# Attention scores kept negated, masked in PSUM by a product, and exponentiated from there

## The chip, the cores and the metric

The kernel runs on one core of one Trainium2 chip. The metric is the device time of one execution in microseconds. The engines are TensorE (PE in the rows, its weight loads PEld), VectorE (DVE), ScalarE (ACT), GpSimd (POOL) and SyncE (SP, which issues the DMAs). Each takes its own instructions in a fixed order; semaphores tie the engines together.

## The reference

One decoder layer on 512 tokens of width 1024, in float32. After a norm and an input projection, two groups of heads run side by side: an RWKV-7 group (8 heads, a recurrence over the tokens, done in chunks of 64) and a sparse-attention group. Their outputs go through an output projection with a residual, then a SwiGLU feed-forward layer and a final norm. The change is in the sparse-attention group, which has 8 query heads of 64 in two groups of 4, each group with its own keys and values, and three branches per head:

- compressed: 31 window tokens made by a small MLP; token t sees a window if the window ends by t; masked softmax, and zero where no window is valid;
- selected: with 8 blocks of 64 tokens and up to 16 chosen, every block is chosen, so this is plain causal attention;
- window: the last 512 tokens, with 512 tokens in all causal attention too, with other keys and values.

```
s = where(valid, q k^T / 8, -1e30);  p = softmax(s);  o = gate_cmp*o_cmp + gate_sel*o_sel + gate_win*o_win
```

## The kernel before

Tokens are tiled by 128 (t = 0..3). The order of the code is: loads, norm and transposition, sixteen projection jobs with their weights split into a high and a low part, RWKV by token tiles (`stage_a`, `stage_b`, `stage_c`), attention by token tiles, output projection, feed-forward, final norm. The code only lists the work; a planner simulates it while the program is built and gives every engine a fixed order by priority and readiness. So attention is woven together with the RWKV tiles that stand ahead of it in the code, and the first part of the output projection with the last attention tile.

PSUM has eight banks, shared by tags: two "s" (scores, some transposes), two "pj" (transposed probabilities, projections), two "ra" and one "rb" (RWKV, projections), one "o" (attention's outputs). In SBUF the probabilities of four heads lie in one tile `prr`, which every pass over four heads reuses.

For a token tile t with n = 128 (t + 1) keys, attention does this:

- Compressed branch (L947 to L969). Per head one product (L949) with the keys' high and low parts side by side, 64 columns. VectorE adds the mask `cneg` to the one half (L953) and the other half to that (L954), takes the maximum over 32 windows (L955), subtracts it (L956); ACT takes the exponential (L957); VectorE sums, inverts and applies the gate (L958 to L960); POOL multiplies by the validity `cvalid` (L961); VectorE normalizes (L962); TensorE transposes (L965), ACT evacuates (L967), TensorE multiplies by the values (L969).
- Selected and window branches (L971 to L1001), in passes over four heads (x = 0..3). For t = 0 and 1 a pass holds both branches (nb = 2), for t = 2 and 3 one. So there are 2 + 2 + 4 + 4 passes and 48 score banks. Per head: two products into an "s" bank (L980 with the keys' high part, L981 with the low part); per branch VectorE computes -(scores + mask) from PSUM into `prr` and its minimum in one instruction (L986, followed by a read of its accumulator), and ACT takes the exponential in place with that minimum as bias and adds up the row (L987); VectorE inverts the sum (L988); POOL scales by the inverse and the gate (L990); TensorE transposes the blocks into a "pj" bank (L993); ACT evacuates (L997), for x = 3 VectorE (L995).
- When a pass is through, the value products add up in "o" (L1001). The pass's transposed probabilities lie in one of two buffers `ptr`. ACT evacuates "o" (L1002).

The causal mask is `negb`, 512 columns of bf16 made at the start by POOL. An f32 product of two f32 operands runs as two instructions; the operands typed as rounded f32 (the scores' ones) take one; a transpose is one. Every product loads its stationary operand anew.

`q` is scaled by 0.125 as it is rotated (`job_qs`), then split and transposed to `qT` (L921 to L934). The helper lines that recur in the rows: L144 and L146 split weights or activations into parts, L163 to L165 are the three products of a projection.

Of the kernel before, what the change touches and what calls it, by code (L numbers as in the profile page):

```python
# [32 lines left out]
def turn_parts(n, bits=12):  # L33
    """1/(2 pi) as n float32 parts of `bits` bits each."""
    from fractions import Fraction
    pi = Fraction(314159265358979323846264338327950288419716939937510582097494459, 10 ** 62)
    rest, parts, unit = 1 / (2 * pi), [], Fraction(1, 2 ** 14)
    for _ in range(n):
        q = int(rest / unit)
        parts.append(float(q * unit))  # L40
        rest -= q * unit
        unit /= 2 ** bits
    return parts
# [3 lines left out]
def hybrid_layer(ctx: ExitStack, tc: tile.TileContext, x, positions, norm_mix, w_in, mu_shift, w0, w2, a0, a2,  # L47
# [26 lines left out]
    def load(src, n):  # L74
        """src: [(128*blocks), n] rows as [128, blocks, n]."""
# [31 lines left out]
    at = 0  # L107
# [40 lines left out]
    def parts(raw, tags=("whi", "wlo"), pool=False, lo_pool=False):  # L148
        """raw [128, blocks, n] -> hi, lo."""
# [17 lines left out]
    def rstd_of(src, cut=()):  # L167
        """1/sqrt(mean(src^2) + eps) over the free axis of [128, D]."""
# [12 lines left out]
    def norm_transposed(src, gain, hT, lT, halves=False):  # L181
        """src(t): [128, D] of token tile t -> hi, lo [128, KB, S] of the normed transpose; by tiles."""
# [24 lines left out]
    def proj_tile(w, c0, m=128):  # L207
        """channels on partitions: m columns of w from c0 -> PSUM [m, S]."""
# [5 lines left out]
    def proj_tok(w, t, m=1):  # L214
        """tokens on partitions: token tiles from t on, the columns of w -> PSUM [128, m * n]."""
# [8 lines left out]
    def mix(p, j, o, m=128):  # L224
        """token shift: p * (1 - mu) + shift(p) * mu."""
# [5 lines left out]
    def rotate(o, src, tab, scale=1.0):  # L231
        """Rotary on the first 16 of each 64 of src [P, t, n, 64] (PSUM) by tab [P, t, 16] -> o; the rest is copied."""
# [14 lines left out]
    # keeps the tensor engine's clock up while the first loads are on their way  # L247
# [9 lines left out]
    # causal mask: the columns from S - 128 - t are those of the token tile t  # L257
    negb = st([128, S], "negb", dtype=BF16)
    POOL.memset(negb, 0.0)
    POOL.affine_select(negb, negb, pattern=[[-1, S]], compare_op=OP.is_ge, fill=MASK, base=S - 128, channel_multiplier=1)  # L260
# [6 lines left out]
    # A_ab: the rows of a chunk's second half have their columns from its middle on, so that the diagonal blocks come first  # L267
# [15 lines left out]
    DVE.tensor_scalar(cneg, cvalid, -MASK, MASK, op0=OP.mult, op1=OP.add)  # L283
# [83 lines left out]
    # pairs of tokens on the contraction: xk[(q d), a, g, m] = token 2m + q  # L367
# [10 lines left out]
    def job_lat(w):  # L378
        # lora: hi and lo of the weights stacked on the contraction, hi in the half q
# [48 lines left out]
    def gate():  # L428
        """sigmoid(g_lat) @ g2, channels on partitions; the last 32 rows: hi, lo, hi by hi, hi, lo on one contraction."""
# [19 lines left out]
    def rsqrt(o, x):  # L449
        """o = 1/sqrt(x), by Newton's steps from a guess that halves the exponent; x [128, n] is positive."""  # L450
# [60 lines left out]
    def inner(a):  # L511
        """A_ab (a = 0) or A_rb (a = 1), transposed, by chunks, masked."""
# [20 lines left out]
    def solve():  # L533
        """A_ab, and a copy whose 32-blocks are on the partitions."""
# [6 lines left out]
    def solve2():  # L541
        """The inverses of the 32-blocks of I - A_ab."""
# [5 lines left out]
        # the rows are independent of each other: the first ones on one engine, the rest on another  # L548
# [11 lines left out]
    def solve4():  # L560
        """(I - A_ab)^-1, transposed, in the place of A_ab: the diagonal blocks, and their product around the block between."""
# [33 lines left out]
    def tok_pair(w, t):  # L595
        """256 columns of w, token tiles t and t + 1 -> [128 tok, 2, 4, 64] in PSUM."""
# [5 lines left out]
    def job_vt(w):  # L602
        """values of the selected and the window branch, tokens on partitions."""
# [6 lines left out]
    def job_ks(w):  # L610
        """keys of the selected (0) and window (1) branch: kA = hi twice, kB = lo twice, channels on partitions."""
# [30 lines left out]
    def job_qs(half):  # L642
        def f(w):
            if half == 0:
                T["qtok"] = st([128, NT, 8, 64], "b8")
            for t in (0, 2):
                rotate(T["qtok"][:, t:t + 2, 4 * half:4 * half + 4], tok_pair(w, t), tab_pair(t), 0.125)
        return f

    def job_cmp1(a, half):  # L650
        """compression of k (a = 0) or v (a = 1): windows -> hidden, half of the contraction."""
        def f(w):
# [10 lines left out]
            # rows: hi, lo of the windows  # L663
# [8 lines left out]
    def hidden(a, b1):  # L672
        """sum of the two rows, transposed; bias, SiLU."""
# [9 lines left out]
    def compressed():  # L683
        """hidden -> one token per window: keys as hi/lo for the scores, values by heads."""
# [69 lines left out]
    rar, abc, rb, rk_, rv, dend, gate_ = (T[n] for n in ("rar", "abc", "rb", "rk", "rv", "dend", "gate"))  # L754
    # the halves of the partitions hold the chunks; "o" operands hold chunk c in the other half, to share a contraction
# [16 lines left out]
    def stage_a(t):  # L772
# [16 lines left out]
        # token layouts; v is centred over each head, which centres y  # L789
# [96 lines left out]
    def stage_c(t):  # L886
        """group norm (y is centred), bonus, gate."""
# [4 lines left out]
        # the sums of the heads of pair i on the partitions from 32i, 16 times each  # L892
# [47 lines left out]
    for t in range(NT):  # L940
# [3 lines left out]
        # the branches' outputs, gated, add up in one bank: [(parity, d), pair of heads, token]  # L944
        po = ps("o", (128, 4, 128))
        # compressed branch
# [191 lines left out]
```

## Time and profile before

| | us |
|---|---|
| device time, three runs | 787.08, 789.80, 790.96; median 789.8 |
| profiled execution: span from first to last instruction | 780.8 |
| profiled execution: its own total | not recorded; the median lies 9.0 above the span |
| TensorE busy, weight loads | 753.5 (96%), 624.1 (80%) |
| VectorE, ACT, POOL busy | 423.9 (54%), 330.3 (42%), 144.4 (18%) |
| mean granted TensorE clock | 0.986 |
| first compressed score product | starts at 230.3 |
| last value product of attention | starts at 372.3 |

Busy time is the union of an engine's instructions; those of TensorE are pipelined and their ends are modelled, so the starts are read beside it. Positions in time are microseconds from the first instruction.

### The profile page before, as it was taken

What the parts mean: (1) busy time and instruction counts of PE and PEld (TensorE: products, weight loads), DVE (VectorE), ACT (ScalarE), POOL (GpSimd) and SP (SyncE); (2) the same over time, 40 slices, a digit from 0 to 9 for tenths busy, and PEclk for the clock granted to TensorE, in tenths of its full rate; (3) what the DMA queues carried; (4) which work ended last, traced back from release to release, by engine and by line L of the source; (5) the groups of instructions that cost most, each with busy time, mean ns of one, the idle gap of its engine ahead of it and who ended that gap; (6) DMA issues with size and microseconds to landing.
All of it is one profiled execution on the core that took longest, in us unless ns stands there. A gap on an engine that the chain in (4) does not pass through costs nothing.

```text
span 780.8 us, 13178 instructions
## 1 busy us (share of the span) xinstructions
PE 753.5 (96%) x5397; PEld 624.1 (80%) x5397; DVE 423.9 (54%) x902; ACT 330.3 (42%) x592; POOL 144.4 (18%) x244
## 2 busy tenths in 40 slices
PE   7999999998989999989999999999999999999996
PEld 6867788988977878756879888888888888888885
DVE  5486689799678878793474133322222323332235
ACT  6399554234277776475343132221221222333224
POOL 3210053068235542252016000000000000000000
PEclk8999999999899999999999999999999999999998
DMA  6622354300030000211353033232233333223302
GB/s 243 166 88 75 108 162 108 108 2 2 3 135 3 3 2 2 83 55 55 108 161 108 1 108 98 67 105 74 89 109 108 107 108 108 76 86 108 107 1 107
DMA packets 51457, 65.40 MB, mean 84 GB/s; under 512 B 3988, under 2 KB 45030, under 8 KB 51398
## 3 DMA queue, kind: packets, MB, share of 16 engines
q1 hardware_dynamic: 51398, 64.57, 25.5%
q8 instruction: 42, 0.69, 0.3%
q14 instruction: 17, 0.14, 0.1%
HBM read 62.47 MB, written 2.10 MB: 83 GB/s over the span
## 4 chain that ended last, share of the span: by engine, by line
PE 81%; DVE 11%; DMA 2%; ACT 2%; issue 2%; POOL 1%; SPq 0%; DVEq 0%; ACTq 0%; POOLq 0%
PE ps_ra L164 9%; PE ps_pj L165 9%; PE ps_ra L163 9%; PE ps_ra L165 9%; PE ps_pj L164 9%; PE ps_pj L163 9%; PE ps_o L1001 3%; DVE wlo L146 2%; PE ps_pj L993 2%; PE ps_s L163 2%; PE ps_s L165 2%; PE ps_s L164 2%; PE ps_s L980 1%; PE ps_ra L798 1%; PE ps_s L981 1%
## 5 line engine op out<-in xcount | busy, mean ns | idle before, releaser
L144 ACT ACTIVATE whi<-wraw 128x1024 fp32r<-128x1024 f32 (+1 forms) x100 | 99.0, 1037 | 148.6 <-PE ps_pj L164 94.3
L146 DVE TENSOR_TENSOR wlo<-wraw,whi 128x1024 fp32r<-128x1024 f32 (+1 forms) x98 | 118.5, 1243 | 65.3 <-ACT whi L144 60.5
L164 PE MATMUL ps_ra<-L,whi 128*128 128x512 f32 (+1 forms) x224 | 87.7, 392 | 0.0
L163 PE MATMUL ps_ra<-L,whi 128*128 128x512 f32 (+1 forms) x224 | 87.6, 391 | 0.0
L165 PE MATMUL ps_ra<-L,wlo 128*128 128x512 f32 (+1 forms) x224 | 87.3, 390 | 0.0
L165 PE MATMUL ps_pj<-L,wlo 128*128 128x512 f32 x216 | 84.6, 392 | 0.8 <-DVE wlo L146 0.6
L163 PE MATMUL ps_pj<-L,whi 128*128 128x512 f32 x216 | 84.5, 391 | 0.5 <-ACT whi L144 0.5
L164 PE MATMUL ps_pj<-L,whi 128*128 128x512 f32 x216 | 84.5, 391 | 0.0
L1082 DVE TENSOR_TENSOR b<-t,ps_ra 128x512 f32<-128x512 f32 x22 | 15.1, 687 | 118.6 <-PE ps_ra L165 118.6
L146 DVE TENSOR_TENSOR L<-b,L 128x512 fp32r<-128x512 f32 x26 | 17.7, 691 | 66.6 <-PE ps_rb L164 62.5
L144 ACT ACTIVATE L<-b 128x512 fp32r<-128x512 f32 x26 | 16.3, 632 | 84.8 <-PE ps_rb L164 69.5
L164 PEld LDWEIGHTS ps_ra<-L,whi 128*128 128x128 f32 (+1 forms) x224 | 41.6, 186 | 9.7 <-issue 0.7
L163 PEld LDWEIGHTS ps_ra<-L,whi 128*128 128x128 f32 (+1 forms) x224 | 41.6, 186 | 9.5 <-DVE b L229 0.4
L165 PEld LDWEIGHTS ps_ra<-L,wlo 128*128 128x128 f32 (+1 forms) x224 | 41.6, 186 | 9.0
L990 POOL TENSOR_SCALAR whi<-whi,m,gates 128x128 f32<-128x128 f32 (+3 forms) x64 | 40.5, 642 | 44.1 <-DVE m L988 30.5
L165 PEld LDWEIGHTS ps_pj<-L,wlo 128*128 128x128 f32 x216 | 40.6, 188 | 9.9 <-DVE wlo L146 1.6
L163 PEld LDWEIGHTS ps_pj<-L,whi 128*128 128x128 f32 x216 | 40.6, 188 | 9.3 <-ACT whi L144 0.9
L164 PEld LDWEIGHTS ps_pj<-L,whi 128*128 128x128 f32 x216 | 40.5, 188 | 8.6 <-issue 0.5
L164 PE MATMUL ps_ra<-wlo,L 128*128 128x256 f32 (+1 forms) x140 | 47.0, 336 | 0.2 <-DVE wlo L146 0.2
L165 PE MATMUL ps_pj<-whi,L 128*128 128x256 f32 (+1 forms) x140 | 47.0, 337 | 0.2 <-DVE L L146 0.2
L163 PE MATMUL ps_ra<-whi,L 128*128 128x256 f32 (+1 forms) x140 | 46.9, 338 | 0.2 <-ACT L L144 0.2
L164 PE MATMUL ps_pj<-wlo,L 128*128 128x256 f32 (+1 forms) x140 | 47.1, 336 | 0.0
(430 smaller groups left out, 1635.2 us busy)
## 6 DMA issues: line engine op xcount, KB each, us to landing
wraw<-in_w_gate_dram SPq DMA_DIRECT2D x11, 1024.0 KB
wraw<-in_w_up_dram SPq DMA_DIRECT2D x11, 1024.0 KB
wraw<-in_w_down_dram SPq DMA_DIRECT2D x11, 1024.0 KB
wraw<-in_w_in_dram SPq DMA_DIRECT2D x9, 1024.0 KB
wraw<-in_w_out_dram SPq DMA_DIRECT2D x4, 1024.0 KB
wraw<-in_w_in_dram SPq DMA_DIRECT2D x6, 512.0 KB
wraw<-in_wk_dram SPq DMA_DIRECT2D x2, 1024.0 KB
wraw<-in_wv_dram SPq DMA_DIRECT2D x2, 1024.0 KB
```

Of the source, the lines that this page charges most:

```text
L144: ACT.activation(hi, src, AF.Copy)
L146: (POOL if pool else DVE).tensor_sub(lo, src, hi.bitcast(F32))
L163: PE.matmul(o, lh, rh, start=start, stop=False)
L164: PE.matmul(o, lh, rl, start=False, stop=False)
L165: PE.matmul(o, ll, rh, start=False, stop=stop)
L798: PE.transpose(p[:, i], src[:, i], ident)
L980: PE.matmul(pS, qT[:, h, ql], kA[:, b0:b0 + nb, g, 0:n], start=True, stop=False)
L981: PE.matmul(pS, qT[:, h, ql], kB[:, b0:b0 + nb, g, 0:n], start=False, stop=True)
L990: POOL.tensor_scalar(pr[:, i], pr[:, i], m[:, i, 2:3], gv[:, 1 + b0 + i, h:h + 1], op0=OP.mult, op1=OP.mult)
L993: PE.transpose(pT[:, j], prr[:, x, j * 128:j * 128 + 128], ident)
L1001: PE.matmul(po[q, 2 * g:2 * g + 2], vtok[:, j % (t + 1), b0 + j // (t + 1), g], pTs[:, par, j], start=False, stop=g == 1 and bs[-1] == 1 a ...
L1082: DVE.tensor_mul(hid[f0 + j], sg, pgu[j][1])
```

## The change

`q` gets the scale -0.125, so that PSUM holds negated scores. The compressed mask `cneg` changes sign. `negb` goes; a bf16 identity and a 128x128 bf16 tile `posb` (0 on and below the diagonal, 1e30 above) come. A third product, identity by `posb`, adds the mask to the last 128 keys of each branch in PSUM; identity by `cneg` opens the bank of the compressed branch, in which the high and low parts now add up in the same 32 columns, by 16 products instead of 8. VectorE takes only a minimum, for both branches in one instruction; the exponential reads PSUM with scale -1 and writes `prr`. Inverse sums are taken for two heads at a time, from one tile `m` for the pass (3 buffers; before one for each head, 5 buffers). The transposes stand behind all four heads of the pass. POOL's product by `cvalid` is left only for t = 0. The diff also deletes comments, which is left out here.

```
@@ masks
-    negb = st([128, S], "negb", dtype=BF16)
-    POOL.memset(negb, 0.0)
-    POOL.affine_select(negb, negb, pattern=[[-1, S]], compare_op=OP.is_ge, fill=MASK, base=S - 128, channel_multiplier=1)
+    identb = st([128, 128], "identb", dtype=BF16)
+    POOL.tensor_copy(identb, ident)
+    posb = st([128, 128], "posb", dtype=BF16)
+    POOL.memset(posb, 0.0)
+    POOL.affine_select(posb, posb, pattern=[[-1, 128]], compare_op=OP.is_ge, fill=-MASK, base=0, channel_multiplier=1)
...
-    DVE.tensor_scalar(cneg, cvalid, -MASK, MASK, op0=OP.mult, op1=OP.add)
+    DVE.tensor_scalar(cneg, cvalid, MASK, -MASK, op0=OP.mult, op1=OP.add)
@@ job_qs
-                rotate(T["qtok"][:, t:t + 2, 4 * half:4 * half + 4], tok_pair(w, t), tab_pair(t), 0.125)
+                rotate(T["qtok"][:, t:t + 2, 4 * half:4 * half + 4], tok_pair(w, t), tab_pair(t), -0.125)
@@ compressed branch
-        pc = ps("s", (128, 8, 2, 32))
+        pc = ps("s", (128, 8, 32))
+        PE.matmul(pc, identb, cneg[:, t, None, :].to_broadcast([128, 8, 32]), start=True, stop=False)
         for h in range(8):
-            PE.matmul(pc[:, h], qT[:, h, ql], kcA[:, h // 4].rearrange("p a n -> p (a n)"), start=True, stop=True)
+            for a in range(2):
+                PE.matmul(pc[:, h], qT[:, h, ql], kcA[:, h // 4, a], start=False, stop=h == 7 and a == 1)
...
-        DVE.tensor_add(sc, pc[:, :, 0], cneg[:, t, None, :].to_broadcast([128, 8, 32]))
-        DVE.tensor_add(sc, pc[:, :, 1], sc)
-        DVE.tensor_reduce(mx, sc, axis=AX.X, op=OP.max)
-        DVE.tensor_sub(sc, sc, mx[:, :, None].to_broadcast([128, 8, 32]))
-        ACT.activation(sc, sc, AF.Exp)
+        DVE.tensor_reduce(mx, pc, axis=AX.X, op=OP.min)
+        DVE.tensor_sub(sc, pc, mx[:, :, None].to_broadcast([128, 8, 32]))
+        ACT.activation(sc, sc, AF.Exp, scale=-1.0)
...
-        POOL.tensor_mul(sc, sc, cvalid[:, t, None, :].to_broadcast([128, 8, 32]))
+        if t == 0:
+            POOL.tensor_mul(sc, sc, cvalid[:, t, None, :].to_broadcast([128, 8, 32]))
@@ selected and window branches
+            m = st([128, 4, 2, 3], "m", 3)
             for x in range(4):
...
-                PE.matmul(pS, qT[:, h, ql], kB[:, b0:b0 + nb, g, 0:n], start=False, stop=True)
-                m = st([128, 2, 3], "m", 5)
+                PE.matmul(pS, qT[:, h, ql], kB[:, b0:b0 + nb, g, 0:n], start=False, stop=False)
+                PE.matmul(pS[:, :, n - 128:n], identb, posb[:, None, :].to_broadcast([128, nb, 128]), start=False, stop=True)
                 pr = prr[:, x, 0:nb * n].rearrange("p (b n) -> p b n", b=nb)
+                DVE.tensor_reduce(m[:, x, 0:nb, 0], pS, axis=AX.X, op=OP.min)
                 for i in range(nb):
-                    DVE.tensor_tensor_reduce(pr[:, i], pS[:, i], negb[:, S - n:S], scale=-1.0, scalar=3e38, op0=OP.add, op1=OP.min, accum_out=m[:, i, 0:1])
-                    ACT.activation(pr[:, i], pr[:, i], AF.Exp, scale=-1.0, bias=m[:, i, 0:1], accum_out=m[:, i, 1:2])
-                DVE.reciprocal(m[:, 0:nb, 2], m[:, 0:nb, 1])
-                for i in range(nb):
-                    POOL.tensor_scalar(pr[:, i], pr[:, i], m[:, i, 2:3], gv[:, 1 + b0 + i, h:h + 1], op0=OP.mult, op1=OP.mult)
+                    ACT.activation(pr[:, i], pS[:, i], AF.Exp, scale=-1.0, bias=m[:, x, i, 0:1], accum_out=m[:, x, i, 1:2])
+                if x % 2 == 0:
+                    continue
+                DVE.reciprocal(m[:, x - 1:x + 1, 0:nb, 2], m[:, x - 1:x + 1, 0:nb, 1])
+                for y in (x - 1, x):
+                    for i in range(nb):
+                        pr = prr[:, y, i * n:i * n + n]
+                        POOL.tensor_scalar(pr, pr, m[:, y, i, 2:3], gv[:, 1 + b0 + i, g * 4 + y:g * 4 + y + 1], op0=OP.mult, op1=OP.mult)
+            for x in range(4):
                 pT = ps("pj", (128, NT, 128))
```

## Rows read from the trace of the kernel before

**Rows 1.** The page, head and first part: engine busy us (share of span) xinstructions.
```profile
span 780.8 us, 13178 instructions
PE 753.5 (96%) x5397; PEld 624.1 (80%) x5397; DVE 423.9 (54%) x902; ACT 330.3 (42%) x592; POOL 144.4 (18%) x244
```

**Rows 2.** The page: the chain that ended last, by engine.
```profile
PE 81%; DVE 11%; DMA 2%; ACT 2%; issue 2%; POOL 1%; SPq 0%; DVEq 0%; ACTq 0%; POOLq 0%
```

**Rows 3.** Windows: stretch, length, busy us of each engine, clock, DMA share, GB/s.
```profile
230.00:350.00 120.00, 116.02 (x1486) 90.60 (x1485) 101.51 (x347) 81.72 (x220) 50.15 (x79) 1.00 0.07 24
230.00:376.00 146.00, 141.77 (x1629) 108.80 (x1628) 112.84 (x375) 95.24 (x247) 55.66 (x86) 1.00 0.08 27
425.00:600.00 175.00, 175.00 (x822) 147.00 (x822) 46.72 (x48) 39.91 (x49) 0.00 (x0) 1.00 0.28 89
```

**Rows 4.** Timeline of TensorE: start, duration, line, operation, shape, count [idle before].
```profile
233.10 0.28 PE L981 MATMUL ps_s<-kB,L 128*128 128x256 f32 x1
233.22 0.32 PE L980 MATMUL ps_s<-b,L 128*128 128x256 f32 x1
...
326.71 0.97 PE L949 MATMUL ps_s<-kcA,L 128*128 128x64 f32 x8
327.61 0.68 PE L862 MATMUL ps_rb<-smask,b 64*64 64x64 f32 x16
...
349.37 1.11 PE L993 MATMUL ps_pj<-ident,whi 128*128 128x128 f32 x8
350.24 0.48 PE L980 MATMUL ps_s<-b,L 128*128 128x512 f32 x1
350.56 0.40 PE L981 MATMUL ps_s<-kB,L 128*128 128x512 f32 x1
350.79 0.40 PE L163 MATMUL ps_ra<-whi,L 128*128 128x512 f32 x1
```

**Rows 5.** Groups by line on VectorE, 228 to 376: busy, mean ns | idle before.
```profile
L986 DVE CUSTOM_DVE_ANT_0 whi<-ps_s,negb 128x128 f32<-128x128 f32 (+3 forms) x64 | 29.1, 484 | 7.8 <-POOL whi L990 2.9 <-PE ps_pj L993 2.7 <-PE ps_s L981 2.0
L988 DVE RECIPROCAL m<-m 128x1 f32<-128x1 f32 (+1 forms) x48 | 7.2, 157 | 6.1 <-ACT whi L987 6.0
L986 DVE DVE_READ_ACCUMULATOR2_ANT m<- 128x1 f32 x64 | 5.2, 82 | 0.0
L804 DVE TENSOR_REDUCE vs<-ps_ra 128x8 f32<-128x512 f32 x3 | 2.0, 680 | 0.0
L955 DVE TENSOR_REDUCE mx<-t 128x8 f32<-128x256 f32 x4 | 1.7, 418 | 0.0
```

**Rows 6.** Timeline of TensorE, 325 to 340, the largest gaps.
```profile
332.39 0.65 PE L1001 MATMUL ps_o<-wlo,b 128*64 128x256 f32 x2 [1.04 <-ACT wlo L997]
...
335.16 1.51 PE L1001 MATMUL ps_o<-wlo,b 128*64 128x256 f32 x10 [0.88 <-DVE wlo L995]
...
339.28 0.44 PE L965 MATMUL ps_pj<-ident,t 128*128 128x128 f32 x2 [0.96 <-DVE t L962]
```

**Rows 7.** Groups by line and shape on ACT, 228 to 376.
```profile
L997 ACT ACTIVATE wraw<-ps_pj 128x512 f32<-128x512 f32 x9 | 5.3, 590 | 4.4 <-PE ps_pj L993 4.4
...
L144 ACT ACTIVATE L<-L 128x512 fp32r<-128x512 f32 x4 | 2.2, 620 | 0.0
```

**Rows 8.** Groups by line on POOL, 228 to 376.
```profile
L961 POOL TENSOR_TENSOR t<-t,cvalid 128x256 f32<-128x256 f32 x4 | 2.7, 672 | 5.2 <-DVE rn L457 3.6 <-DVE den L958 1.6
```

**Rows 9.** Timeline of TensorE, VectorE and ACT at the start of t = 3.
```profile
328.99 0.48 PE L980 MATMUL ps_s<-b,L 128*128 128x512 f32 x1
...
332.19 0.68 DVE L986 CUSTOM_DVE_ANT_0 whi<-ps_s,negb 128x512 f32<-128x512 f32 x1
332.97 0.50 PE L980 MATMUL ps_s<-b,L 128*128 128x512 f32 x1
333.06 0.71 ACT L987 ACTIVATE whi<-whi,m 128x512 f32<-128x512 f32 x1
...
339.56 0.60 PE L993 MATMUL ps_pj<-ident,whi 128*128 128x128 f32 x4
```

## The prediction

> **What bounds the kernel now.** The page comes first: TensorE is busy 96% of the span, no other engine over 54% [rows 1], and the chain that ended last is 81% TensorE, 11% VectorE [rows 2]. That is an average over stages, so I then read the stretches. In the table of windows [rows 3] attention lies between 230 and 376 us, woven together with the last RWKV tiles; there the reader is to see TensorE busy 141.8 of 146 us, so idle 4.2, at granted clock 1.00, and VectorE at 112.8 (77%; 85% up to 350). From 425 to 600 TensorE is busy 175.00 of 175.00, so no wait is left there in which a later start could vanish: what attention loses or gains reaches the end one for one.
>
> A busy TensorE need not be a full one, since ends are modelled. So I read starts [rows 4]. Eight transposes begin at 349.37 and the next product at 350.24: 0.109 us each. Eight L949 products (64 columns) take from 326.71 to 327.61: 0.1125 each, as long as 128 columns do, so it is not their columns that pace them but, as the nearest explanation, the load of their 128x128 stationary operand. A 512-column score product takes 0.23 (350.56 to 350.79), a 256-column one 0.12 (233.10 to 233.22). These spacings stand back to back through most of the stretch: TensorE is really near full.
>
> One rule speaks against that reading. The Trainium skill, Trainium Kernel Development and Optimization, Best Practices, says to judge the distance to the limit by how busy weight loads are, not by matmul busy time, as matmuls are pipelined. By weight loads TensorE is at 108.8 of 146, 75%. By the busy row the stretch has 4 us to spare, by the rule some 37; the spacings side with the busy row, but the rule feeds rival D.
>
> **The change, part by part.**
>
> *Mask product on the selected and window branches (TensorE, added).* Each head and pass gets a third product: 8 heads each for t = 0 and 1 (two branches at once, 256 columns), 16 each for t = 2 and 3 (128 columns). At 0.12, 16 x 0.12 = 1.9 us; the 32 of 128 columns at the spacing of the f32 transposes, 0.109, 3.5 us. bf16 operands occur in no matmul of this trace. Lower bound of the 32: half the 256-column spacing, 0.06, 1.9 us. Upper bound: a score product behind transposes starts its successor after 0.32 (350.24 to 350.56) instead of 0.23, so a change of format may cost 0.09; at both sides of 48 products that is 8.6 us more. I take 5.4, as 0.109 is the nearest row for a changed 128x128 operand.
>
> The Trainium skill, TensorE: Matmul & The Clock Gate, Weight-path perf modes, says that 128 weights of a type other than FP32 are loaded by a faster path. If so, the 32 products go towards the 0.06 end and the sum falls by 1.6 us; no run here shows it.
>
> *Compressed branch (TensorE, added).* Per token tile, 8 products of 64 columns become 16 of 32, and one 256-column mask product is added. If the stationary operand paces them, the 8 more cost 8 x 0.1125 = 0.9; with the mask 1.02 per tile, 4.1 for four. If narrow products could go closer, say at the 0.06 of above, it is 8 x 0.06 + 0.12 = 0.6, 2.4 for four. I take 4.1.
>
> TensorE's sum: 5.4 + 4.1 = 9.5 us (1.9 + 1.9 + 2.4 = 6.2 at least; 9.5 + 8.6 = 18 at most).
>
> *VectorE (removed).* The fused add-and-minimum L986 costs 29.1 us in 64 pieces, and its accumulator reads 5.2: 34.3 [rows 5]. The plain minimum is priced by the reductions there: 0.68 for 512 from PSUM, 0.418 for 256, and 0.55 for 384 by interpolation: 24 x 0.68 + 16 x 0.55 + 8 x 0.418 = 28.5. Reciprocals: 48 become 24, at 0.158 a gain of 3.8. Compressed: two additions over 256 columns go in each tile, priced as the reduction of that size, 0.418: 3.3. Total -13 us; bounds -9 (an accumulator read of 0.08 still behind each of the 48) and -13, since no pass of these rows over 256 columns goes under 0.41. VectorE does not end the stretch, so this counts for nothing by itself; its worth is what it takes out of TensorE's 4.2 us of idle.
>
> *Idle that may go* [rows 6]. Three gaps hold 2.9 of it. 1.04 us at 332 stands behind an ACT evacuation that is itself queued behind L144, waiting for weights from DMA; nothing here changes that. 0.88 at 335 stands behind a VectorE copy, 0.96 at 339 behind the end of the compressed chain, which gets shorter by the two additions and, for t > 0, the POOL product of 0.67 us [rows 8]. I take back 1.5; bounds 0 and 4.2.
>
> *Exponential from PSUM (ACT).* 64 activations as before, plus the same accumulator reads. A 512-column copy costs 0.59 from PSUM and 0.62 from SBUF [rows 7]; so -0.03 each, -2 us (bounds 0 and -2), on an engine busy 95 of 146 [rows 3]: nothing.
>
> *Score banks held longer (an added wait).* There are two "s" banks. Before, VectorE's pass frees a bank; after, ACT's exponential does. At t = 3 the ring is already tight [rows 9]: scores start at 328.99, their minimum ends at 332.87, and the next scores enter that bank at 332.97; the exponential of the same head ends at 333.77. So each turn of the ring grows by 0.9 us here. Behind the waiting score product queue all of TensorE's products, and behind those the evacuations. With 16 heads in two banks, 8 turns: 0 if other products fill the time, 7.2 if each turn counts. Up to 325 RWKV products fill it; at t = 3 only own transposes and value products do. I take +0.5, because the written order comes from a planner that simulates these waits and can put work in between, and keep 7.2 for a rival.
>
> *The rest.* Reciprocals in pairs make the first head of a pair wait about one more exponential (0.71 [rows 9]) before POOL scales it; POOL is busy 56 of 146 us [rows 3] and its waits lie off TensorE unless a transpose is next. Transposes now come after all four heads in program order; in the trace the heads of t = 3 are scored in pairs from 328.99 and 332.97 on, and the first transposes of four blocks stand at 339.56 [rows 9], so the order is hardly new: 0, up to 1 if POOL is late. The wait for the old contents of the probability tile moves from VectorE (2.9 + 2.7 us of its idle time [rows 5]) to ACT, where evacuations queue behind it; if that cover goes, it is of the same size. At the start POOL makes two tiles of 128 columns instead of one of 512, in the time in which TensorE waits for the first data: 0. The signs of q and cneg cost nothing.
>
> **Sum.** +9.5 - 1.5 + 0.5 = +8.5 us, nearly all on TensorE. Against the profiled span: 780.8 + 8.5 = 789.3. The execution's own total is not given; the timed runs (787.1 to 791.0) are 6.3 to 10.2 above the span, the median 9.0. With 9.0 around the span: 798.
>
> **Rivals.** A difference under 0.5% (3.9 us) could not be told from none: below 785.9 counts as faster, above 793.7 as slower.
>
> B, the ring decides: each of the 8 turns at t = 3 takes its 0.9 us, and t = 2 loses half that: 7.2 + 3.6 on top of 798 is 808. For: the 0.1 us between release and reuse. Against: until 325 there is other work, and the waits are known to the planner.
>
> C, the extra products fall into holes: low TensorE prices (6.2) and all 4.2 of idle gone: +2, 792. For: VectorE, which gets lighter, is at 85% until 350. Against: the largest of the gaps in rows 6 hangs on DMA, not on VectorE.
>
> D, VectorE paces and the products only look full: the 13 us it sheds come off, and the 9.5 are hidden: 777. It decides only if the products' true need, with the addition, is under (146 - 13) of 146 us, that is if over 22 of 142 busy us are pretence. For: VectorE 85%, and the weight-load share. Against: the spacings of rows 4.
>
> **How the numbers follow.** Forecast 0.50 (794 to 802), B 0.20, C 0.16, D 0.14. Slower 0.70, same 0.16, faster 0.14. Cutting half of D below and some of B above gives 786 to 809.
>
> **What would show it.** Right: TensorE gains some 84 products; L949 takes 1.8 us a tile instead of 0.9; mask products are spaced by about 0.11; the stretch from the first compressed product to the last value product grows by 8 to 9 us, TensorE idle in it is 2 to 4 us, VectorE's time in it falls to about 100 us; after 425 nothing differs but the offset. Wrong: mask spacing at 0.06 or 0.2; TensorE idle over 8 us, waiting for ACT exponentials (B); a stretch that is shorter, with fewer gaps (C, D); a granted clock under 1.00 in it.

## The result, and the profile after

The changed kernel takes 792.92 us (median of 19 runs, 788.86 to 796.68), the kernel before, run beside it, 789.8 (median of 19 too). The ratio is 1.0053, with a 95% interval of 1.0033 to 1.0073: 4.2 us slower, 2.6 to 5.8. A second set of runs gave 1.0063 (1.0037 to 1.0089). The forecast, 8.5 us slower, had the direction and twice the size. In absolute time 792.92 lies inside the wide range (786 to 809), but under the middle one (794 to 802) that got a chance of 0.50, a little under the 793.7 from which the forecast would have counted it as slower, and next to rival C's 792. The 9.0 between span and total was no property of an execution: every timed run of after lies 1.7 to 1.8 above its own span, so the profiled execution of before took some 782.5, and the 9.0 was mostly its distance from the median.

First the head of the page of after and its chain by engine, to be held against [rows 1, 2]:

```profile
span 795.0 us, 13230 instructions
PE 768.8 (97%) x5481; PEld 636.6 (80%) x5481; DVE 419.2 (53%) x790; ACT 328.6 (41%) x592; POOL 143.3 (18%) x242
PE 83%; DVE 10%; issue 2%; ACT 2%; DMA 2%; POOL 1%; SPq 0%; ACTq 0%; DVEq 0%; POOLq 0%
```

TensorE has the 84 products more, VectorE 112 instructions less. The spans lie 14.2 us apart, more than four times as far as the medians (3.1): the profiled execution of before was one of its shortest, that of after one of its longest. So the stretches have to be compared one by one. The windows ahead of attention, from its first compressed product to its last value product, and behind it; before:

```profile
0.00:230.30 230.30, 215.25 (x1920) 183.68 (x1921) 171.62 (x372) 121.50 (x194) 73.69 (x150) 0.96 0.33 102
230.30:372.70 142.40, 138.17 (x1612) 105.82 (x1610) 110.32 (x373) 94.54 (x245) 55.66 (x86) 1.00 0.08 28
372.70:780.80 408.10, 400.04 (x1869) 334.55 (x1868) 141.95 (x158) 114.29 (x153) 15.08 (x8) 0.99 0.28 93
```

and after, with one more window of 3 us inside the last:

```profile
0.00:237.80 237.80, 221.74 (x1920) 189.90 (x1921) 171.94 (x372) 122.28 (x194) 73.36 (x151) 0.93 0.32 99
237.80:385.50 147.70, 145.69 (x1696) 110.58 (x1694) 105.73 (x261) 91.94 (x245) 54.85 (x83) 1.00 0.08 27
385.50:795.00 409.50, 401.39 (x1869) 336.11 (x1868) 141.52 (x158) 114.40 (x153) 15.06 (x8) 0.99 0.28 93
...
425.00:428.00 3.00, 3.00 (x14) 3.00 (x15) 1.69 (x4) 2.24 (x5) 3.00 (x2) 0.50 0.00 0
```

The 14.2 are 7.5 + 5.3 + 1.4. The first part is the clock: length times granted clock is 230.3 x 0.96 = 221.1 and 237.8 x 0.93 = 221.2, the same work as far as two digits of the clock can tell (0.005 of 230 is 1.2 us), and the same 1920 product instructions stand in both. The last is the clock as well: 3 us at 0.50, which is the level of 1.2 GHz, lose 1.5. TensorE had been idle for 1.67 us shortly before (up to 423.67); in before it is idle for the same 1.67 us at that place (up to 410.89), and the granted clock stays at 1.00 behind it. What is left is attention, +5.3 us at clock 1.00 (inside the interval of 2.6 to 5.8), and that is what the experiments below are read by.

To see what fills those 5.3 us, I added up, from all TensorE records of the stretch, the time from each start to the next by the role of the product, with marked idle taken out:

| us in attention | before | after | difference |
|---|---|---|---|
| mask products on selected and window | 0 | 5.2 | +5.2 |
| compressed branch, scores with mask | 3.6 | 7.3 | +3.7 |
| scores, two products a head | 23.5 | 23.9 | +0.4 |
| transposes of probabilities | 18.5 | 17.9 | -0.6 |
| value products | 24.5 | 23.8 | -0.7 |
| RWKV, projections, other compressed | 68.0 | 67.8 | -0.2 |
| idle | 4.2 | 1.6 | -2.6 |
| sum | 142.3 | 147.5 | +5.2 |

So the added products cost about what they were priced at, 5.2 + 3.7 and the 0.4 of their neighbours, the score products: 9.3 for 9.5. Of those 9.3 us, 4.1 came back in two places: 2.6 in idle and 1.5 in products that were not changed. The timeline of TensorE in after shows the prices (start, duration, line, operation, shape, count):

```profile
237.93 0.27 PE L950 MATMUL ps_s<-cneg,identb 128*128 128x256 bf16 x1
237.96 1.94 PE L953 MATMUL ps_s<-kcA,L 128*128 128x32 f32 x16
239.74 0.37 PE L985 MATMUL ps_s<-b,L 128*128 128x256 f32 x1
...
338.68 0.23 PE L987 MATMUL ps_s<-posb,identb 128*128 128x128 bf16 x1
338.72 0.42 PE L985 MATMUL ps_s<-b,L 128*128 128x384 f32 x1
338.98 0.34 PE L986 MATMUL ps_s<-kB,L 128*128 128x384 f32 x1
...
348.05 0.23 PE L987 MATMUL ps_s<-posb,identb 128*128 128x128 bf16 x1
348.21 1.51 PE L1010 MATMUL ps_o<-wlo,b 128*64 128x256 f32 x10
...
350.98 0.23 PE L987 MATMUL ps_s<-posb,identb 128*128 128x128 bf16 x1
351.05 0.61 PE L1002 MATMUL ps_pj<-ident,whi 128*128 128x128 f32 x4
```

and in before two score products with no mask product ahead of them:

```profile
303.84 0.34 PE L980 MATMUL ps_s<-b,L 128*128 128x384 f32 x1
304.01 0.34 PE L981 MATMUL ps_s<-kB,L 128*128 128x384 f32 x1
```

The reader is to look at starts. Sixteen L953 products of 32 columns take from 237.96 to 239.74, 0.111 each: half the columns of [rows 4] at the same price, so 1.8 us a tile, as forecast. A mask product of 128 columns holds up its successor by 0.04 if that is a score product (338.68 to 338.72), by 0.07 before a transpose (350.98 to 351.05) and by 0.16 before a value product (348.05 to 348.21). The 0.04 is not the whole price: the score product behind it starts its partner 0.26 later (338.72 to 338.98), against 0.17 behind another score product in before (303.84 to 304.01). So 0.09 more stands in the row of the score products. With the 16 of 256 columns, which go up to 0.21, the mean over all 48 is 5.2 / 48 = 0.108. The sign that was named, a spacing of about 0.11, holds as a mean only.

VectorE in after by line (busy us, mean ns | idle before it), against [rows 5]:

```profile
L989 DVE TENSOR_REDUCE m<-ps_s 128x1 f32<-128x384 f32 (+3 forms) x48 | 27.9, 596 | 10.3 <-PE ps_s L987 9.9
L994 DVE RECIPROCAL m<-m 128x2 f32<-128x2 f32 (+1 forms) x24 | 4.0, 167 | 6.2 <-ACT whi L991 6.2
L957 DVE TENSOR_REDUCE mx<-ps_s 128x8 f32<-128x256 f32 x4 | 1.7, 414 | 0.5 <-PE ps_s L953 0.5
```

The minimum costs 27.9 (forecast 28.5) in place of 34.3. VectorE's instructions in attention, each with its own duration, add up to 130.1 us in before and 116.5 in after: 13.5 less, as forecast. Yet its busy time, a union, falls only from 110.3 to 105.7 and not to 100, since in before more of these durations overlap (19.7 us, in after 10.8). A saving that is added up from durations can't be taken off a union. VectorE now waits 9.9 us for the mask product. And the waits of TensorE in the stretch (waiting line, what it waited for: us in total, times, longest):

```profile
PE ps_pj L1002 <- POOL whi L998: 0.6, 2, 0.4
PE ps_ra L828 <- DVE wlo L823: 0.4, 1, 0.4
PE ps_o L1010 <- ACT wlo L1006: 0.3, 1, 0.3
PE ps_s L985 <- ACT whi L991: 0.2, 1, 0.2
```

Score products that wait for a bank that the exponential still reads stand in the last line: 0.2 us in all. Rival B, the ring, is not what is seen here. The three gaps of [rows 6] are gone as well.

### The profile page after: what moved, and what is told of

It is laid out like the page before. It is cut to its first block, busy times and chain, and to the rows that moved or that the text cites. A ratio compares the mean times of both kernels' runs of the same rounds, so it can differ in the third digit from the quotient of the medians.

```text
span 795.0 us, 13230 instructions
## 1 busy us (share of the span) xinstructions
PE 768.8 (97%) x5481; PEld 636.6 (80%) x5481; DVE 419.2 (53%) x790; ACT 328.6 (41%) x592; POOL 143.3 (18%) x242
## 3 DMA queue, kind: packets, MB, share of 16 engines
q1 hardware_dynamic: 51398, 64.57, 25.3%
## 4 chain that ended last, share of the span: by engine, by line
PE 83%; DVE 10%; issue 2%; ACT 2%; DMA 2%; POOL 1%; SPq 0%; ACTq 0%; DVEq 0%; POOLq 0%
PE ps_ra L164 9%; PE ps_ra L165 9%; PE ps_ra L163 9%; PE ps_pj L163 9%; PE ps_pj L164 9%; PE ps_pj L165 9%; PE ps_o L1010 2%; DVE wlo L146 2%; PE ps_pj L1002 2%; PE ps_s L163 2%; PE ps_s L164 2%; PE ps_s L165 2%; PE ps_s L985 1%; DMA wraw<-in_w_in_dram 1%; PE ps_s L986 1%
## 5 line engine op out<-in xcount | busy, mean ns | idle before, releaser
L144 ACT ACTIVATE whi<-wraw 128x1024 fp32r<-128x1024 f32 (+1 forms) x100 | 99.0, 1037 | 148.1 <-PE ps_pj L164 94.3
L163 PEld LDWEIGHTS ps_pj<-L,whi 128*128 128x128 f32 x216 | 40.6, 188 | 9.4 <-ACT whi L144 0.9
L163 PE MATMUL ps_pj<-whi,L 128*128 128x256 f32 (+1 forms) x140 | 47.7, 344 | 0.0
L165 PE MATMUL ps_pj<-whi,L 128*128 128x256 f32 (+1 forms) x140 | 47.5, 340 | 0.0
```

What stands on the lines that cost most here:

```text
L144: ACT.activation(hi, src, AF.Copy)
L163: PE.matmul(o, lh, rh, start=start, stop=False)
L165: PE.matmul(o, ll, rh, start=False, stop=stop)
```

## The experiments

All times of attention are those of the profiled execution, from the first compressed product to the last value product; ratios are to the kernel before, run beside it. Where a stretch holds time at a granted clock of 0.50, the length without half of that time stands in brackets.

| kernel | attention us | idle in it | ratio | 95% interval |
|---|---|---|---|---|
| before | 142.4 | 4.2 | | |
| after | 147.7 | 1.6 | 1.0053 | 1.0033 to 1.0073 |
| again | 147.6 | 1.6 | 1.0063 | 1.0037 to 1.0089 |
| cmp_old | 148.1 | 4.0 | 1.0089 | 1.0059 to 1.0119 |
| cmp_only | 135.7 (134.0), other content | 1.3 | 0.9984 | 0.9962 to 1.0005 |
| mask_none | 146.1 | 5.0 | 1.0062 | 1.0040 to 1.0084 |
| recip | 149.2 | 0.9 | 1.0094 | 1.0063 to 1.0125 |
| inter | 151.6 (149.9) | 3.0 | 1.0132 | 1.0100 to 1.0163 |
| hold | 147.0 | 6.4 | 1.0069 | 1.0038 to 1.0100 |
| ring | 147.5 | 0.7 | 1.0090 | 1.0055 to 1.0124 |
| none_ring | 147.7 (146.0) | 4.4 | 1.0082 | 1.0050 to 1.0114 |
| cmpold_ring | 147.2 | 3.0 | 1.0058 | 1.0024 to 1.0092 |
| pool4 | 183.7, at a mean clock of 0.92 | 19 | 1.0589 | 1.0547 to 1.0631 |
| pool4_b | 271.7, much of it at 0.50 | | 1.1678 | 1.1628 to 1.1729 |

**again.** The changed kernel as it is, beside the next three.

> The changed kernel once more, to have a second profile beside a granted clock of its own. In the first, attention (first compressed product to last value product) takes 147.6 us against 142.4 before, and 7.6 us more were already lost ahead of it, where the clock stood at its lower level for longer. Theory T (TensorE paces attention; its added products cost some 8 us there, of which its idle gives back 2 to 3; what differs ahead of attention is the clock of that one execution): attention again takes 147 to 148.5 us, and the offset at its start is another one than 7.6, following the clock. Rival O (the planner's order was changed ahead of attention too, and costs time there): the offset at the start of attention stays at 7 to 8 us.

The stretch is the same to 0.1 us, idle too. That sets the scale: attention of one program repeated. The other half of the expectation failed: attention starts at 237.8 again, as rival O had it, so this run alone can't tell the order ahead of attention from the clock there, 0.93 both times. Two later runs can, windows from the start to attention's first product:

```profile
0.00:230.60 230.60, 215.34 (x1921) 183.76 (x1922) 171.44 (x372) 121.81 (x194) 73.42 (x151) 0.96 0.32 102
0.00:235.30 235.30, 219.48 (x1921) 187.81 (x1922) 172.24 (x372) 121.93 (x194) 73.85 (x150) 0.94 0.32 100
```

The first is cmpold_ring, which changes nothing of after ahead of attention and starts it at 230.6 with before's clock; the second is hold, which has before's code there and starts it at 235.3 at a lower clock. Length times clock is 221.4 and 221.2 again. So the start follows the clock and not the change. Nor has after the lower clock as a rule: the mean granted clock is 0.981 over its 19 runs, over the 8 of again and over the 19 of before beside again.

**cmp_old.** After, with the compressed branch of before:

```
-        PE.matmul(pc, identb, cneg[:, t, None, :].to_broadcast([128, 8, 32]), start=True, stop=False)
...
-            for a in range(2):
-                PE.matmul(pc[:, h], qT[:, h, ql], kcA[:, h // 4, a], start=False, stop=h == 7 and a == 1)
+            PE.matmul(pc[:, h], qT[:, h, ql], kcA[:, h // 4].rearrange("p a n -> p (a n)"), start=True, stop=True)
...
+        DVE.tensor_add(sc, pc[:, :, 0], cneg[:, t, None, :].to_broadcast([128, 8, 32]))
+        DVE.tensor_add(sc, pc[:, :, 1], sc)
...
```

> The changed kernel with the compressed branch of before (8 products of 64 columns, mask added by VectorE in two additions; signs kept negated). T: TensorE loses 8 x 0.1125 us and the mask product in each of four tiles, 3.7 us; VectorE gets back 3.3 us; the kernel is 2.5 to 3.7 us faster than the changed one, so within 2 us of before. Rival V (VectorE's relief is what pays, so its return costs): same as the changed kernel or slower. Rival W (small products are hidden behind the loads of others): same.

It takes 3.7 us of products out and gets no faster: attention 148.1, idle 4.0 instead of 1.6. So the number of T failed; V and W, which had it the same or slower, stand. Of the idle, 2.4 us is a score product behind the exponential that holds its bank, against 0.2 in after:

```profile
PE ps_s L985 <- ACT whi L991: 2.4, 2, 1.8
```

Another 2.1 us are in the value products, 25.8 for 23.8, though this edit doesn't touch them: the planner gave the whole stretch another order.

**cmp_only.** Before, with only the compressed branch of after (mask product, 16 products, maximum from PSUM).

> The kernel before with the compressed branch alone changed (mask product into PSUM, 16 products of 32 columns, reduction and subtraction from PSUM, POOL's product by the validity only for t = 0); signs stay positive. T: +3.7 us on TensorE less about 1 of idle: 2 to 4 us slower than before. V: 1 to 3 us faster than before. W: same.

Its edit is the diff of that branch on the kernel before, with the bf16 identity:

```
+        PE.matmul(pc, identb, cneg[:, t, None, :].to_broadcast([128, 8, 32]), start=True, stop=False)
...
+                PE.matmul(pc[:, h], qT[:, h, ql], kcA[:, h // 4, a], start=False, stop=h == 7 and a == 1)
...
+        DVE.tensor_reduce(mx, pc, axis=AX.X, op=OP.max)
```

It adds some 4 us of products and is not slower, 0.9984; T had said 2 to 4 us slower. Its attention is not comparable as it stands, since none of the 36 output-projection products, 8.9 us in before, are woven into it; they follow it. From the start of attention to the end of the span it takes 782.3 - 231.0 = 551.3 us, before 780.8 - 230.3 = 550.5. Of the 551.3, 1.7 are lost at half clock:

```profile
234.40:237.80 3.40, 3.40 (x52) 3.06 (x50) 2.73 (x16) 2.65 (x12) 1.82 (x4) 0.50 0.03 7
```

So added products need not add time, in both directions of this edit. Why is open: both edits move VectorE's two additions a tile together with the products, so the runs can't tell products that are hidden (W) from a shorter chain on VectorE that pays for them (V). Idle of 1.3 against 4.2 in before would fit V; an edit that moves the products alone was not run. It is the fastest of the kernels with any part of the change, and can't be told from before.

**mask_none.** After without the mask product, so without the causal mask on the selected and window branches.

```
-                PE.matmul(pS[:, :, n - 128:n], identb, posb[:, None, :].to_broadcast([128, nb, 128]), start=False, stop=True)
```

> The changed kernel without the mask products of the selected and window branches; it leaves out the causal mask there. T: the 48 products take 32 x 0.066 + 16 x 0.119 = 4.0 us in the changed kernel's profile, and the score product behind each starts its partner 0.09 us later where it had followed a score product (about half of them, 2 us): 4 to 6 us faster than the changed kernel, so 0 to 2 us under before. Rival R (the score banks' ring, held until the exponential has read them, sets the pace at t = 2 and 3): under 2 us faster, since each turn of the ring gets only 0.07 us shorter.

5.2 us of products go, and attention falls by 1.6; the ratio doesn't move. Idle rises by 3.4 to 5.0. The waits of TensorE in it:

```profile
PE ps_s L985 <- ACT whi L990: 2.3, 3, 1.3
PE ps_s L985 <- DVE L L868: 1.6, 1, 1.6
PE ps_pj L969 <- DVE t L966: 0.6, 1, 0.6
```

The first line is the wait that rival B named, a score product behind the exponential that holds its bank: 2.3 us, against 0.2 in after. Of the 3.4 us more idle that is 2.1; 1.6 is a wait for VectorE in the RWKV part (L868). So most of the time of the mask products is taken by waits, the bank's the largest of them: the two costs do not add up. T's 4 to 6 us failed; R's number, under 2 us, came out.

**hold.** To price the held bank alone: before, with one short ScalarE read of each score bank behind its exponential.

```
+                ACT.activation(hold[:, 0:nb], pS[:, :, 0], AF.Copy, scale=m[:, nb - 1, 1:2])
                 DVE.reciprocal(m[:, 0:nb, 2], m[:, 0:nb, 1])
```

> The kernel before with one more read of each score bank by ACT behind the head's exponential (one column per branch, scaled by the row sum so that it can't come earlier), so that a bank is held as long as in the changed kernel; it adds 48 ACT instructions of some 0.25 us, 12 us to an engine busy 95 of 146. R1: 3 to 6 us slower than before. R2, R3, T: within 1.5 us of before.

No product is added, and attention takes 4.6 us more, the number of R1 (the held bank alone; the letters are spelled out under recip). Of these, 2.2 are idle; the rest stands in the spacing of score and value products, which the planner ordered anew. TensorE's waits:

```profile
PE ps_s L980 <- ACT hold L989: 1.6, 3, 1.0
PE ps_s L949 <- ACT hold L989: 1.3, 1, 1.3
PE ps_o L1003 <- ACT wraw L999: 1.0, 1, 1.0
```

2.9 us wait for a bank; the third line is an evacuation behind a ScalarE that has more to do. The 48 reads cost ScalarE 11.9 us, which after doesn't have, so 4.6 is an upper reading of what held banks cost in before, not the measure of it in after:

```profile
L989 ACT ACTIVATE hold<-ps_s,m 128x1 f32<-128x1 f32 (+1 forms) x48 | 11.9, 256 | 0.6
```

**recip, inter.** After with the reciprocal and the scaling taken for each head at once (recip), and with the transposes moved back into the loop over heads as well (inter):

```
-                if x % 2 == 0:
-                    continue
-                DVE.reciprocal(m[:, x - 1:x + 1, 0:nb, 2], m[:, x - 1:x + 1, 0:nb, 1])
+                DVE.reciprocal(m[:, x, 0:nb, 2], m[:, x, 0:nb, 1])
...
-            for x in range(4):          # inter only: no second loop
                 pT = ps("pj", (128, NT, 128))
```

> The changed kernel with the inverse of the row sum taken for each head by itself, as before, not for two at a time. So far the compressed branch alone, put into the kernel before, cost nothing (ratio 0.998, 0.996 to 1.001) although it adds 3.7 us of TensorE, and the changed kernel without its mask products is as slow as with them (1.006 both): theory T, that added products are the cost, does not hold for these. Theory R (the new order of waits in the selected and window branches costs some 5 us: banks held until the exponential has read them, pairs of heads, transposes behind four heads) splits into R1 (held banks), R2 (pairs) and R3 (transposes behind four heads). R2: 2 to 4 us faster than the changed kernel. R1, R3: same within 1.5 us.

> The changed kernel with the inverse for each head and with the transposes back in the loop of the heads, as before; bank held until the exponential, mask product and compressed branch as changed. R3: 2 to 5 us faster than recip. R1: same as recip within 1.5 us. T (products): same as recip.

Both have a longer attention than after, 149.2 and 151.6, where R2 had said 2 to 4 us less for recip and R3 another 2 to 5 less for inter; both numbers failed. Of its 151.6 inter loses 1.7 us at half clock, in this window:

```profile
348.60:352.00 3.40, 3.40 (x17) 1.47 (x19) 2.27 (x8) 0.78 (x2) 2.68 (x3) 0.50 0.69 278
```

The interval of inter, 1.0100 to 1.0163, lies clear of that of after; the one of recip overlaps it. All three run the same products, so look at the windows of recip:

```profile
237.60:386.80 149.20, 148.21 (x1695) 110.60 (x1693) 106.03 (x285) 92.96 (x245) 53.16 (x83) 1.00 0.08 27
```

TensorE is busy 148.2 us with what takes 145.7 in after. The busy row alone can't say why; starts can. A pass of the last tile has 8 value products, each of two instructions, so 16 in the rows. In recip these stand in two groups:

```profile
374.24 0.65 PE L1006 MATMUL ps_o<-wraw,b 128*64 128x256 f32 x2
374.81 1.09 PE L998 MATMUL ps_pj<-ident,whi 128*128 128x128 f32 x8
...
377.81 1.94 PE L1006 MATMUL ps_o<-wraw,b 128*64 128x256 f32 x14
379.68 0.66 PE L998 MATMUL ps_pj<-ident,whi 128*128 128x128 f32 x4
```

and in after one pass is a single group:

```profile
365.72 1.95 PE L1010 MATMUL ps_o<-wlo,b 128*64 128x256 f32 x16
367.60 0.73 PE L165 MATMUL ps_ra<-whi,L 128*128 128x512 f32 x2
```

Split, the 16 take (374.81 - 374.24) + (379.68 - 377.81) = 2.44 us; whole, 367.60 - 365.72 = 1.88. It isn't the break alone that costs. Added up from all records, from a group's first start to its successor's, most groups of 2 take 0.58, but so do groups of 4; 6 and 8 take 1.01, 10 and 12 take 1.44, 14 and 16 take 1.88. The price goes in steps of four, and a break that leaves 2 over pays for a step it doesn't fill. Over the stretch the value products stand in 26 groups in recip, 24 in inter, 23 in before and 19 in after, and take 26.3, 26.4, 24.5 and 23.8 us (inter's with 1.3 us lost to the half clock). In recip that is 2.5 us over after, more than its whole loss of 1.5, for its idle is 0.7 less. That after's grouping comes from the new order of the code is not shown: cmp_old and cmpold_ring keep that order, and their value products stand in 25 and 24 groups and take 25.8 and 25.3 us.

**ring.** After, with every second head of the last tile scored into the two banks that RWKV no longer needs.

```
-                pS = ps("s")[:, 0:nb * n]
+                pS = ps("ra" if t == 3 and x % 2 else "s")[:, 0:nb * n]
```

> The changed kernel with the scores of the odd heads of the last token tile (t = 3) in the two RWKV banks, which are free by then: four score banks instead of two there. R1: 2 to 4 us faster than the changed kernel, the waits of score products for the exponential (2.4 us in the changed kernel) gone. T, R2, R3: same within 1.5 us.

Four banks give nothing: 147.5, idle 0.7. With 0.2 us of bank waits in after there was nothing to give; the 2.4 us that the expectation names are cmp_old's.

**none_ring, cmpold_ring.** The theory was then that either bound, products or the two banks, holds attention at 147, and that lifting both would show it: mask_none and cmp_old, each with the line of ring.

> The changed kernel without the mask products of the selected and window branches (it leaves out the causal mask there) and with four score banks at t = 3: both suspects taken away together. Each alone left attention (first compressed product to last value product) where it was: 146.0 us without the mask products, with TensorE idle 5.0 us, half of it waiting for exponentials; 147.4 us with four banks, idle 0.7; 147.6 us changed, idle 1.6. Theory TR (two bounds of nearly the same height, TensorE's products and the ring of two score banks; lifting one shows the other): attention 141 to 144 us, 3 to 5 us faster than the changed kernel in all. Rival N (neither counts; the planner's order around the last RWKV tile does): 145 to 148 us, within 1.5 us of the changed kernel.

> The changed kernel with the compressed branch of before and four score banks at t = 3. With the branch alone put back, attention took 148.1 us, TensorE idle 4.0, of which 2.4 for exponentials. TR: 3.7 us less of products and 1.8 us less of ring: attention 143 to 145.5 us, 2 to 4 us faster than cmp_old. N: 147 to 149 us, same as cmp_old.

none_ring takes 147.7 us, of which 1.7 are lost at half clock:

```profile
237.00:240.40 3.40, 3.40 (x47) 2.83 (x48) 2.42 (x8) 2.67 (x9) 1.24 (x3) 0.50 0.03 7
```

That leaves 146.0, as in mask_none, so the two added banks gave nothing and the theory's number fell. Its longest wait is again a score product behind an exponential, in one of the added banks:

```profile
PE ps_ra L985 <- ACT whi L990: 1.3, 1, 1.3
PE ps_pj L969 <- DVE t L966: 1.2, 1, 1.2
```

cmpold_ring takes 147.2, 0.9 less than cmp_old. Both lie where rival N, the planner's order, had put them (145 to 148 and 147 to 149). But neither says whether the two banks still bind up to t = 2, where the RWKV tiles need all others, or whether the planner's order has the say.

**pool4, pool4_b.** One pool of four banks for scores, transposes and projections in place of two and two, in after and in cmp_only.

```
-PS_BUFS = {"ra": 2, "rb": 1, "pj": 2, "s": 2, "o": 1}
+PS_BUFS = {"ra": 2, "rb": 1, "s": 4, "o": 1}                 # and tag "pj" becomes "s"
```

> The changed kernel with one pool of four PSUM banks for scores and transposed probabilities (and for all other uses of the two tags) instead of two and two: the ring gets loose at every token tile, TensorE's products stay. TR: attention 145 to 147.5 us, since TensorE is full there; within 2 us of the changed kernel, either way. If the ring had been the only bound: 142 to 144 us.

> The kernel before with the changed compressed branch (cmp_only: ratio 0.998 to before) and with the pool of four banks: the version that should be fastest by what was found, since bank, VectorE and products are each off their limit. TR: attention's start to the end of the kernel as cmp_only (551 us) or up to 3 us less; 0 to 4 us faster than before. Against: the projections ahead use the same banks and may be ordered worse.

Both were meant to lift the ring everywhere and answer nothing: the planner ordered the whole stretch anew, with transposes at the head of TensorE's queue behind POOL,

```profile
PE ps_s L1003 <- POOL whi L999: 10.5, 9, 2.1
```

and attention took 183.7 and 271.7 us, in part because the granted clock fell in it: its mean is 0.92 in pool4's, which is worth some 14 of the 183.7.

## Why the prediction was right, and where its size was off

*Mask products.* Forecast 5.4, measured 5.2 in their own spacing and some of the 0.4 by which the score products rise. The mean of 0.108 was near, its reason only partly right: not one spacing like that of the f32 transposes, but 0.04 to 0.21 according to columns and successor. Both that were named, a cheap bf16 product and a change of format at 0.09, are seen side by side: 0.04 before a score product, and 0.09 more behind that one. The Trainium skill, TensorE: Matmul & The Clock Gate, Weight-path perf modes, has 128 weights of a type other than FP32 loaded by a faster path; the trace agrees (the loads of L987 and L953 in after: minimum, median, maximum in ns), 96 for bf16 against 192 for f32:

```profile
L987 PEld LDWEIGHTS <-identb x48: 95/96/98, 240.1 to 373.8; 128*128 128x128 bf16 x48
...
L953 PEld LDWEIGHTS ps_s<-kcA,L x64: 190/192/192, 237.9 to 342.8; 128*128 128x128 f32 x64
```

*Compressed branch.* Forecast 4.1, measured 3.7, at 0.111 a product for 0.1125.

*Idle that may go.* Forecast -1.5, measured -2.6. The gaps behind the compressed chain and behind VectorE's evacuation went, but also the one that I put down to ACT and DMA and left in.

*Held banks.* Forecast +0.5; in after the wait is 0.2 of the 1.6 idle. As a term of the sum it was right, and the reason given, that other work fills the time, fits mask_none, where the wait rises to 2.3 when the mask products go. It is not cheap in itself: hold, with 11.9 us of reads beside it, shows 2.9 us of it and takes 4.6 more.

*The rest.* Here stands the failed step: "the order is hardly new: 0, up to 1 if POOL is late". It was judged by where the first transposes stand, and bounded on the side of loss only. In after it came out as a gain: unchanged kinds of products take 1.5 us less (value -0.7, transposes -0.6, others -0.2). With the order undone (inter), attention at full clock is 7.5 us over before, where the forecast had said 8.5; inter has 1.7 us of bank waits in that, so it is no clean measure either. And since cmp_old has the new order without the gain in value products, the cause of the gain stays open: it can be the new order, or one grouping among several that the planner may arrive at. So 8.5 to 5.2 is: products 0.2 (9.5 to 9.3), idle 1.3 (-1.5 to -2.8, without the bank's 0.2), held banks 0.3, the rest 1.5. Idle and the rest are nearly all of these 3.3 us.

*VectorE and the exponential.* VectorE's reductions cost what was forecast and counted for nothing by themselves, as said; the sign "about 100 us" took a sum of durations off a union and failed. The exponential's 512-column form takes less from PSUM, 690 ns on average over 16, than from SBUF in before, 718 (one of them 0.71 us in [rows 9]). Rival D (VectorE paces) is refuted: VectorE sheds work and attention grows. (Its condition was summed wrongly: 142 + 9.5 - 133 is 18.5, not 22.) Rival C had its half on idle more right than the forecast, 2.6 of 4.2 gone, and its cheap products wrong, 9.3 for 6.2; the measured growth of 5.2 lies halfway between its 2 and the 8.5.

*The signs.* The 84 product instructions and the 1.8 us a tile came as named. The stretch grew by 5.3 and not by 8 to 9, idle is 1.6 and not 2 to 4, VectorE 105.7. Of the signs of being wrong none came, if the mask spacing is taken as the mean. That the direction is right owes something to luck: the same prices said 2 to 4 us slower for cmp_only, which is not slower.

*After 425 nothing differs but the offset:* so it is, apart from the 3 us at half clock.

**Open.** The sum closes, but it describes one order and is no law. cmp_only adds 4 us of products for nothing, mask_none takes 5.2 out for 1.6 in attention and nothing in the ratio, cmp_old 3.7 for nothing. The Trainium skill, Trainium Kernel Development and Optimization, Best Practices, would judge the room by weight loads, and these were busy only 110.6 of 147.7 us; that cmp_only's products cost nothing fits such room, but no run here turned it into a gain. That the added products explain the 5.2 us is therefore the account of the trace, and not shown by taking them away: with them gone, attention still takes 146 to 148 us, with more waits for score banks and other chains in it. Whether that is the two banks at t = 0 to 2 or the planner's order for each program, no run here separates. Nor was the new order of transposes and reciprocals tried alone on the kernel before, nor the compressed branch's products without its lighter VectorE.

## What to carry to other kernels

A sum of added products forecasts the time only while nothing else waits behind the same engine: take the products out once, and see whether their time comes back or another wait moves in. Price a small product by the neighbours that it will have, not by one spacing. And an edit that only reorders, here to run the heads of a pass through before their transposes, deserves a price of both signs, since it can change how like products are grouped: here a pass of 16 value instructions took 2.44 us in two groups and 1.88 in one.

## What had not been expected of the hardware

- The compressed mask, a 256-column bf16 product that opens a bank, delays the start of its successor by only 0.03 us (237.93 to 237.96), whereas sixteen f32 products of 32 columns behind it take 0.111 each, as those of 64 columns did [rows 4].
- Splitting 16 value instructions into 2 and 14 costs 0.56 us, shown as busy time: 2 cost as much as 4, and 14 as much as 16. A stretch can be 99% busy (148.2 of 149.2 in recip) and yet hold time that another order saves.
- The granted clock goes with larger differences than the change makes: the runs of one kernel, cmpold_ring, spread from 787.2 us at a mean of 0.988 to 795.9 at 0.976. The mean alone doesn't fix the time (one run of 790.5 us has 0.937). Times of single executions tell little here; the stretch of the program that was profiled twice repeated to 0.1 us at clock 1.00.
